# Where the queries' inverse norms are applied, and where some operands are let in, in a two-layer hybrid attention block

## The chip, the cores and the metric

The kernel runs on one core of one Trainium2 chip. The metric is device microseconds of one execution. A core has several engines that work side by side, each with its own queue of instructions: TensorE (PE in the profile; PEld is its weight loads) multiplies matrices, VectorE (DVE) and ScalarE (ACT) do elementwise work, GpSimd (POOL) does elementwise work and issues some transfers, and SyncE (SP) issues the other transfers. The engines wait for each other by semaphores. Matrix products land in PSUM banks, everything else lies in SBUF.

## The reference, cut to what matters

The input is 512 tokens of width 1024, with 16 learned meta tokens ahead of them: T = 528. Two layers run one after the other, each like this:

```python
h = rms_norm(x, norm_g)
q, k, v, gate_a, u_b, gate_b, q_idx, k_idx, w_idx, merge = split(h @ w_in)
q = rope(rms_norm(q, qn_g)); k = rope(rms_norm(k, kn_g))     # 8 heads of 64 for q, one for k and v
attn = indexer_sparse_attention(q, k, v, rope(q_idx), rope(k_idx), w_idx, k_top=128)
y_a = (attn * silu(gate_a)) @ w_a
y_b = (multiscale_pool(u_b, ...) * silu(gate_b)) @ w_b
g_a, g_b = split(sigmoid(merge))
x = x + (g_a * y_a + g_b * y_b) @ w_out
```

In `indexer_sparse_attention` eight index heads give every query a score for each key that it may see (chunks of 64 tokens, causal by chunk), the 128 keys with the largest scores are kept, and each of the eight heads does a softmax over the kept keys alone. `rms_norm(q)` divides a query of one head by its root mean square, so 1/rms is one number per token and head. Everything is float32.

## The kernel before

**Numbers.** A float32 product is made of three TensorE passes over operands split in two parts of the format float32r: high by high, low by high, high by low. So each weight and each activation appears as a high part, made by a cast on ACT (`high`, L177; `hhi`, `ahi`), and a low part, made by a subtraction of the high part on DVE (`low`; on POOL for some of `hlo`). A weight chunk is 256 columns of w_in, in two halves of 128x1024.

**Order.** TensorE and DVE execute in the order in which the program writes their instructions. ACT, POOL and SP are ordered by the framework's scheduler. The program arranges its text with four devices:

- `prep_q` is a list of steps that turn a loaded chunk into operands. `w_prep_enqueue` adds a chunk's steps; `prep_one` does the next. `group_done`, called after each group of matmuls, and `end()` in `mix_gates` take steps from it by a count. A plain chunk has three steps: `high(0)`; `low(0)` with `high(1)`; `low(1)`. Other chunks have their low parts made by an accumulating transfer of POOL (`minus`, L191 and L192, and `plus`, L196).
- `later(fn, n)` puts a step n groups of matmuls behind.
- `fill` holds generators of steps (index scores, attention) that are let in beside the dense products. They are paid by a credit which grows by a rate for each group: `R_ATT` (L30) is that rate in the attention, one number for each layer.
- `sel` holds the steps of the top-k: a maximum of eight (`dve.max`) and a replacement of these eight, 16 rounds, two query tiles interleaved. They are let in when the DVE time counted so far lies below the TensorE time counted so far. `ensure(i)`, called before the logits of query tile i, forces what is left of the top-k that this tile needs, in one burst.

**Buffers.** SBUF tiles rotate in named pools. Those that matter: "L", six buffers of 128x544 (logits `lt`, index scores `r`, split queries `qs`, pool sums `us`, the gates' weight sum, fetched sheets `hsheet`); "tt", six of 128x272 (RoPE terms `t1`, `t2`, squares `sq`, `th`, `c`, `p1`); "B", eight (split queries of the index `qi`, attention queries `qq`, `pw`, and from the fifth gate group on the gates `ta`). A tile waits until the readers of the tile that had its buffer are done.

**Stages of a layer.** Norm; key, value and index key with the first index queries; the other index queries; gate_b and pool branch; `queries(0)`, gate_a, `queries(1)`; the pool branch's output `zb` (`dense`, copied by ACT at L1148); the merge gates (`mix_gates`); the attention branch's output (`ahi`, `alo` times w_a); w_out. The index scores, the top-k and the attention are let in from the queries' stage to the end of the merge gates.

**The queries.** `q_post(t, ps, normed, dst)` (L555 on) takes one token tile's four heads from PSUM: two DVE products for RoPE; with `normed`, ACT's square (L567), a DVE sum, a DVE addition and POOL's power −1/2 (`rq`, L433) give 1/rms; POOL adds the two products (L572); one group later DVE multiplies by `rq` and ACT casts the high part (`qs`, L581), then DVE makes the low part, TensorE transposes and ACT copies to `qq` (L590).

**A unit of attention** is one tile of 128 queries and two heads; there are 16 units in a layer. `logits` does the matmuls; `soft` adds the mask and takes the minimum in one DVE instruction for each head (`lt`, `mn`; the logits come with their sign turned, so the minimum is the largest), then ACT's exponential with scale −1 and the minimum as bias (L680), summing to `sm`; `scale` takes the reciprocal `rs` on DVE, multiplies on ACT (`lt`, L691) and puts the 16 meta columns, multiplied on DVE, into `pm`; `turn` transposes on TensorE and ACT copies to `pt` (L707); `values` multiplies by v. Meta columns of all heads are multiplied in one go after a tile's fourth unit (`meta_turn`). In layer 0 the meta tokens' own attention (`meta_attn`) follows at the end.

**Merge gates.** Eight groups q = 0 to 7 of seven products each (a Strassen-like scheme over two halves of the tokens and of the width), in the order a11, a12, s2, s1, s3, s4, a22; a product is 12 matmuls. Some operands are sums of activations; two of the four sheets go to memory early and are fetched late: `fetch(w, g)` (L826, a transfer on SP), `high` (L832, ACT) and `low` (DVE), in the order fetch(1,0), fetch(1,1), high and low of both, fetch(0,0), fetch(0,1), each after a group of the `zb` stage, then `last_sum` with the high and low parts of the (0,·) pair.

**w_a.** When a query tile's attention is done, `splits` makes its `ahi` on ACT (L1161) and puts it in `alo_q`; `alos` makes all that is there on DVE. It is called in the last gate group between the product s4 and its `end()`, and after the gates. w_a's matmuls use high by high first, `alo` last.

Of the kernel before, what the change touches and what calls it, by code (L numbers as in the profile page):

```python
# [8 lines left out]
F32 = mybir.dt.float32  # L9
# [8 lines left out]
T = 528  # L18
# [8 lines left out]
HB = 272  # L27
NCOL = 968
LB = 6
R_ATT = (1.8, 1.7)  # L30
FULL = 1.0
CAP = 1.5
W0 = 3
# [54 lines left out]
def tile_block(ctx: ExitStack, tc: tile.TileContext, x, meta, w_in, pool_w, w_a, w_b, w_out, rows, hgain, c_tab, out):  # L88
# [63 lines left out]
    def w_tile():  # L152
        return wpool.tile([128, 1024], F32R, tag="w", name="w", bufs=8)

    def w_prep_enqueue(eng=dve):
        c = W["prep"]
        if c >= len(chunks):
            return
        W["prep"] += 1
        kt = chunks[c][0][0].shape[1]  # L160
        cols = 2048 // kt
        ready[c] = {}
        if c in mixed:
            prep_q.extend(mixed_prep(c))
            return
        parts = ready[c] = ([], [])

        def split(which):
            t = w_tile().rearrange("p (k e) -> p k e", e=cols)
            parts[which].extend(t[:, k] for k in range(kt // 2))  # L170
            return t

        his = {}

        def high(s):
            his[s] = split(0)
            act.copy(his[s], raws[c][s])  # L177

        def low(s):
            eng.tensor_sub(split(1), raws[c][s], f(his[s]))  # L180
            if s == 1:
                del raws[c]
                w_load()

        def second():
            low(0)
            high(1)

        def minus(s):
            t = split(1)  # L190
            act.activation(t, raws[c][s], AF.Copy, scale=-1.0)  # L191
            gp.dma_start(t, raws[c][s], accum_op=OP.add)  # L192

        def plus(s):
            t = split(0)
            act.copy(t, raws[c][s])  # L196
            if s == 1:
                del raws[c]
                w_load()

        if c in by_dma:
# [199 lines left out]
    Ck = one.tile([128, 5, 64], F32, name="Ck")  # L401
    Sk = one.tile([128, 5, 64], F32, name="Sk")
    BV = one.tile([128, 4, 2, 64], F32, name="BV")

    def small(n, name):
        return tmp.tile([128, n], F32, tag=f"sm{n}", name=name, bufs=6)
# [145 lines left out]
        later(third, 2)  # L552
        later(trans, 3)

    def q_post(t, ps, normed, dst):  # L555
        s, m = TOK[t]
        p3 = ps[:m, :256].rearrange("p (h d) -> p h d", h=4)
        t1 = tmp.tile([128, HB], F32, tag="tt", name="t1", bufs=6)
# [6 lines left out]
        if normed:  # L565
            sq = tmp.tile([128, HB], F32, tag="tt", name="sq", bufs=6)
            act.activation(sq[:m, :256], ps[:m, :256], AF.Square, scale=HD ** -0.5)  # L567
            ss = small(4, "ss4")
            dve.tensor_reduce(ss[:m], sq[:m, :256].rearrange("p (h d) -> p h d", h=4), axis=AX.X, op=OP.add)
            rq = small(4, "rq")  # L570
            inv_rms(rq[:m], ss[:m], dve)
        gp.tensor_tensor(t1[:m, :256], t1[:m, :256], t2[:m, :256], op=OP.add)  # L572
        if normed:
            qs = tmp.tile([128, 544], F32R, tag="L", name="qs", bufs=LB)[:, :512].rearrange("p (h c) -> p h c", h=4)
# [1 line left out]
            qs = tmp.tile([128, 4, 128], F32R, tag="P", name="qs", bufs=3)  # L576

        def second():
            if normed:
                dve.tensor_tensor(v1, v1, rq[:m, :, None].to_broadcast([m, 4, 64]), op=OP.mult)  # L580
            act.copy(qs[:m, :, 0:64], v1)  # L581

# [66 lines left out]
    def attention(ensure):  # L649
        st, pvs, pms = {}, {}, {}  # L650

        def logits(u):
            i, j = divmod(u, 4)
            if j == 0:
                ensure(i)
                pms[i] = tmp.tile([128, NH, 16], F32, tag="pm", name="pm")
            st[u] = []
            for hh in range(2):
                h = 2 * j + hh
                qS = QS[i, h // 4][:, h % 4, :]  # L660
                for pi, (o, w) in enumerate(KPARTS[i]):
                    ps = bank("a")
                    pe.matmul(ps[:, :w], qS, KK[:, 0, o:o + w], start=True, stop=False)
                    pe.matmul(ps[:, :w], qS, KK[:, 1, o:o + w], start=False, stop=True)
                    st[u].append((hh, pi, o, w, ps))

        def soft(u):
            i, j = divmod(u, 4)
            n = NK[i]
            mn, sm = small(2, "mn"), small(2, "sm")  # L670
            L = {}
            for hh, pi, o, w, ps in st[u]:
                if pi == 0:
                    L[hh] = tmp.tile([128, 544], F32, tag="L", name="lt", bufs=LB)
                e = min(w, n - o)
                dve.tensor_tensor_reduce(L[hh][:, o:o + e], ps[:, :e], SC[i][:, n - 1::-1] if i == 0 else SC[i][:, o:o + e], 1.0,
                                         3e38 if pi == 0 else mn[:, hh:hh + 1], op0=OP.add, op1=OP.min,
                                         accum_out=mn[:, hh:hh + 1])
            for hh in range(2):
                act.activation(L[hh][:, :n], L[hh][:, :n], AF.Exp, scale=-1.0, bias=mn[:, hh:hh + 1],  # L680
                               accum_out=sm[:, hh:hh + 1])
            st[u] = L, sm

        def scale(u):
            i, j = divmod(u, 4)
            n = NK[i]
            L, sm = st[u]
            rs = small(2, "rs")
            dve.reciprocal(rs, sm)
            for hh in range(2):  # L690
                act.activation(L[hh][:, 16:n], L[hh][:, 16:n], AF.Copy, scale=rs[:, hh:hh + 1])  # L691
                dve.tensor_scalar(pms[i][:, 2 * j + hh, :], L[hh][:, 0:16], rs[:, hh:hh + 1], None, op0=OP.mult)
            st[u] = L

        def turn(u):
# [99 lines left out]
    def sums_of_h(l, s0, n2):  # L795
# [25 lines left out]
        back = {}  # L821

        def fetch(w, g):
            t = back[w, g] = tmp.tile([128, 544], F32, tag="L", name="hsheet", bufs=LB)[:, :2 * n2].rearrange(
                "p (k c) -> p k c", k=2)
            dma(t, far[:, w, g])  # L826

        def high(w, g):
            if w == 0 and not t1_:
                t1_.append(one.tile([128, 2, 4, T // 2], F32R, tag="Alo", name="hsum1"))  # L830
            k = slice(2 * g, 2 * g + 2)
            act.copy(H[0][:, k, c1] if w else t1_[0][:, 0, k, :n2], back[w, g])  # L832

        def low(w, g):
            k = slice(2 * g, 2 * g + 2)
            hi, lo = [H[s][:, k, c1] if w else t1_[0][:, s, k, :n2] for s in range(2)]
            dve.tensor_sub(lo, back.pop((w, g)), f(hi))
# [25 lines left out]
    def mix_gates(zb, ta, s0, n2, operands, splits, alos):  # L863
        base = popped[0] - progress[W["use"]]
        end_ = [None]
        for q in range(8):
# [17 lines left out]
            def end():  # L884
                done[0] += 1
                group_done()
                while prep_q and popped[0] < base + 9 * q + LEAD + done[0] * 9 // 7:
                    prep_one()

            def gate(eh, t, src, in_sheet):  # L890
# [36 lines left out]
            total(1, 1, U, p5)  # L927
            end()
            product(S, "s4", False)
            if q == 7:  # L930
                alos()
            end()
            product(U, "a22", False)
            total(0, 1, S, u)
            gate(1, 0, U[:, :n2], False)
# [47 lines left out]
    for l in range(2):  # L983
# [20 lines left out]
        for what, t in (("q", 1), ("q", 2), ("k", 3), ("k", 4), ("q", 3), ("q", 4)):  # L1004
# [21 lines left out]
        def queries(g):  # L1026
            w = chunk()
            for t in range(0 if l == 0 else 1, 5):
# [5 lines left out]
                later(lambda t=t, ps=ps, dst=dst: q_post(t, ps, True, dst), 1)  # L1034
                group_done()


# [282 lines left out]
```

## Time and profile before

| | |
|---|---|
| median of three executions | 783.36 us (783.23 to 786.67) |
| the profiled execution | 784.69 us |
| its span | 782.9 us |
| mean granted TensorE clock | 0.997 |
| busy: TensorE, DVE, ACT, POOL | 755.2, 569.2, 468.2, 194.6 us |
| TensorE idle in the span | 27.7 us |

Times in the profile are microseconds from the start of the span, of one execution. A row of a group gives line, engine, operation, the tiles written and read by name, the shape, the count, then total busy time and mean nanoseconds of one, then the idle time of the engine just before and what ended it. Many instructions go through one recording helper and have its line, L60; they are told apart by tile. A row of the waits names the engine that waits and the work that ended the wait.

### The profile page before, as it was taken

The numbers are of one execution on the slowest core, as the hardware profiler recorded it, in microseconds if no ns is written. First come the engines' busy times: TensorE is split into PE (matmuls) and PEld (weight loads), VectorE is DVE, ScalarE is ACT, GpSimd is POOL, SyncE is SP. The second block draws the span as 40 slices with busy tenths as digits, with TensorE's granted clock in tenths as the row PEclk, the third lists the DMA queues.
The fourth block names the chain that finished last, engine by engine and source line by source line (L and its number), as shares of the span: only waits on it lengthen the run. The fifth ranks groups of instructions, "written<-read, shape, count | busy, mean of one in ns | idle before, by whom it ended". The sixth has DMA issues, their size and how long they took to land.

```text
span 782.9 us, 15738 instructions
## 1 busy us (share of the span) xinstructions
PE 755.2 (96%) x5989; PEld 717.9 (92%) x5989; DVE 569.2 (73%) x1434; ACT 468.2 (60%) x1044; POOL 194.6 (25%) x240
## 2 busy tenths in 40 slices
PE   7999999999999999899999999999999899999998
PEld 5999999999889999899999989988868899999998
DVE  6866787788897876784367568868788878858531
ACT  5677844737677787543245796555577687863420
POOL 6551164324000000053345411751400000004300
PEclk9999999999999999999999999999999999999999
DMA  9547585675022112544431678668711222127311
GB/s 297 174 103 194 141 197 136 142 196 123 28 81 83 54 56 82 158 141 136 136 109 57 161 163 206 144 148 206 175 50 55 63 85 70 56 92 234 121 57 41
DMA packets 73260, 96.95 MB, mean 124 GB/s; under 512 B 3632, under 2 KB 58192, under 8 KB 73184
## 3 DMA queue, kind: packets, MB, share of 16 engines
q1 hardware_dynamic: 67424, 74.97, 30.2%
q0 software_dynamic: 5760, 20.97, 14.7%
q8 instruction: 47, 0.77, 0.4%
q14 instruction: 29, 0.24, 0.1%
HBM read 66.41 MB, written 8.55 MB: 96 GB/s over the span
## 4 chain that ended last, share of the span: by engine, by line
PE 80%; DVE 11%; ACT 3%; POOL 2%; DMA 2%; issue 1%; SPq 0%; POOLq 0%; DVEq 0%; ACTq 0%
PE d L60 65%; PE a L60 11%; PE v L60 4%; DVE w L60 1%; DVE sc L60 1%; DVE t L60 1%; DMA hsheet<-far 1%; DVE nf L60 1%; DVE m L60 1%; POOL rq L433 1%; DVE hlo L60 1%; DVE alo L60 1%; ACT sq L567 1%; DVE ta L60 1%; DVE ss L60 0%
## 5 line engine op out<-in xcount | busy, mean ns | idle before, releaser
L60 PE MATMUL d<-hhi,w 128*128 128x256 f32 (+3 forms) x1408 | 291.4, 297 | 0.0
L60 PEld LDWEIGHTS d<-hhi,w 128*128 128x128 f32 x1408 | 227.0, 189 | 7.7 <-issue 2.3
L60 PE MATMUL d<-hlo,w 128*128 128x256 f32 (+3 forms) x704 | 193.8, 294 | 0.6 <-POOL hlo L1187 0.6
L60 PE MATMUL d<-w,hhi 128*128 128x256 f32 (+2 forms) x928 | 145.7, 286 | 3.8 <-ACT w L177 2.7
L60 PEld LDWEIGHTS d<-hlo,w 128*128 128x128 f32 x704 | 132.8, 189 | 3.2 <-POOL hlo L1187 0.8
L60 PEld LDWEIGHTS d<-w,hhi 128*128 128x128 f32 (+1 forms) x928 | 125.7, 186 | 8.0 <-ACT w L177 3.1
L60 DVE TENSOR_TENSOR w<-raw,w 128x512 fp32r<-128x512 f32 (+1 forms) x130 | 109.8, 855 | 2.7 <-ACT w L216 1.3
L1187 POOL TENSOR_TENSOR hlo<-ta,hhi 128x256 fp32r<-128x256 f32 (+1 forms) x32 | 31.3, 992 | 310.9 <-PE d L60 296.0
L60 PE MATMUL d<-w,hlo 128*128 128x256 f32 (+2 forms) x464 | 85.4, 282 | 0.0
L60 PE MATMUL d<-hsum,w 128*128 128x264 f32 (+1 forms) x576 | 78.7, 288 | 3.4 <-DVE w L60 3.4
L60 PEld LDWEIGHTS d<-hsum,w 128*128 128x128 f32 x576 | 72.9, 191 | 4.8 <-DVE w L60 3.8
L60 PEld LDWEIGHTS d<-w,hlo 128*128 128x128 f32 (+1 forms) x464 | 68.1, 187 | 0.4
L192 POOL DMA_DIRECT2D w<-raw x40 | 36.6, 934 | 101.9 <-ACT w L191 80.4
L216 ACT CAST w<-raw 128x512 fp32r<-128x512 f32 x96 | 57.0, 627 | 6.9 <-DVE raw L60 6.9
L60 DVE MATCH_REPLACE8 sc<-m,sc 128x400 f32<-128x400 f32 (+2 forms) x100 | 54.3, 549 | 0.0
L60 DVE MAX8 m<-sc 128x8 f32<-128x400 f32 (+2 forms) x100 | 52.7, 557 | 0.7
L60 PE MATMUL d<-mhi,w 128*128 128x272 f32 (+2 forms) x192 | 48.4, 330 | 0.2 <-ACT zb L1148 0.2
L191 ACT ACTIVATE w<-raw 128x1024 fp32r<-128x1024 f32 x40 | 41.4, 1059 | 8.6 <-PE d L60 8.6
L60 DVE SCALAR_TENSOR_TENSOR sc<-r,wsg,sc 128x144 f32<-128x144 f32 (+3 forms) x56 | 32.4, 582 | 16.3 <-ACT r L607 13.9
L680 ACT ACTIVATE lt<-lt,mn 128x144 f32<-128x144 f32 (+3 forms) x64 | 36.5, 574 | 10.2 <-DVE mn L60 10.2
L607 ACT ACTIVATE r<-a,wab 128x272 f32<-128x272 f32 (+2 forms) x80 | 35.8, 497 | 10.8 <-PE a L60 10.8
L196 ACT CAST w<-raw 128x1024 fp32r<-128x1024 f32 x40 | 41.5, 1054 | 0.0
(195 smaller groups left out, 1335.3 us busy)
## 6 DMA issues: line engine op xcount, KB each, us to landing
raw<-in_w_in_dram SPq DMA_DIRECT2D x72, 512.0 KB, 3.8
w<-raw POOLq DMA_DIRECT2D x40, 512.0 KB, 5.9
raw<-in_w_out_dram SPq DMA_DIRECT2D x16, 512.0 KB, 3.4
kept<-res SPq DMA_DIRECT2D x16, 264.0 KB, 2.6
res<-kept SPq DMA_DIRECT2D x16, 264.0 KB, 5.3
raw<-in_w_branch_b_dram SPq DMA_DIRECT2D x8, 512.0 KB, 4.5
raw<-in_w_branch_a_dram SPq DMA_DIRECT2D x8, 512.0 KB, 3.7
xt<-in_x_dram SPq DMA_DIRECT2D x4, 512.0 KB, 5.4
```

The lines of the kernel that those rows point to most:

```text
L60: return fn(*a, **k)
L191: act.activation(t, raws[c][s], AF.Copy, scale=-1.0)
L192: gp.dma_start(t, raws[c][s], accum_op=OP.add)
L196: act.copy(t, raws[c][s])
L216: act.copy(t[:, 0], blk[src[n]])
L433: gp.tensor_tensor(o, o, half, op=OP.pow)
L567: act.activation(sq[:m, :256], ps[:m, :256], AF.Square, scale=HD ** -0.5)
L607: act.activation(r[:, n - 1::-1] if i == 0 else r[:, o:o + e], ps[:, :e], AF.Relu, scale=wab[:, i, h:h + 1])
L680: act.activation(L[hh][:, :n], L[hh][:, :n], AF.Exp, scale=-1.0, bias=mn[:, hh:hh + 1], accum_out=sm[:, hh:hh + 1])
L1187: gp.tensor_sub(hlo[:, j, a:a + n], d, f(hhi[:, j, a:a + n]))
```

## The change

Six edits, all of them in the order or the place of work:

1. `R_ATT` of layer 0 goes from 1.8 to 1.95.
2. In one plain chunk of each layer (the one taken up after the last key tile, `("k", 4)`) both casts are one step, ahead of both low parts: `casts_first=True`.
3. For the 128-token tiles the queries are no longer multiplied by 1/rms. It is kept in `RQ` [128, 4 tiles, 8 heads], and `NR` = −`RQ` is made once for each tile. The minima are multiplied by `RQ` (one DVE instruction of 128x2 for each unit) and the exponential's scale is `NR` in place of −1. Both heads' exponentials follow that multiplication. The meta tokens' queries keep the multiplication.
4. The meta columns of `pm` are multiplied on POOL instead of DVE.
5. `fetch(0,0)` uses a buffer of "B" instead of "L"; `fetch(0,1)` two of "tt", with two transfers, two casts and two subtractions; fetch(1,·) stay in "L".
6. In the last gate group, after its fifth product, all that is left in `prep_q` is done; `alos` comes after s4's `end()` and leaves the two youngest parts for the call after the gates.

```diff
-R_ATT = (1.8, 1.7)
+R_ATT = (1.95, 1.7)
...
-    def w_prep_enqueue(eng=dve):
+    def w_prep_enqueue(eng=dve, casts_first=False):
...
+        def highs():
+            high(0)
+            high(1)
+
+        if casts_first:
+            prep_q.extend((highs, lambda: low(0), lambda: low(1)))
-        if c in by_dma:
+        elif c in by_dma:
...
+    RQ = one.tile([128, 4, NH], F32, name="RQ")
+    NR = one.tile([128, 4, NH], F32, name="NR")
...
-    def q_post(t, ps, normed, dst):
+    def q_post(t, ps, normed, dst, g=0):
...
-            inv_rms(rq[:m], ss[:m], dve)
+            inv_rms(rq[:m] if t == 0 else RQ[:, t - 1, 4 * g:4 * g + 4], ss[:m], dve)
...
-            if normed:
+            if normed and t == 0:
                 dve.tensor_tensor(v1, v1, rq[:m, :, None].to_broadcast([m, 4, 64]), op=OP.mult)
...
                 pms[i] = tmp.tile([128, NH, 16], F32, tag="pm", name="pm")
+                dve.tensor_scalar(NR[:, i], RQ[:, i], -1.0, None, op0=OP.mult)
...
+            dve.tensor_tensor(mn, mn, RQ[:, i, 2 * j:2 * j + 2], op=OP.mult)
             for hh in range(2):
-                act.activation(L[hh][:, :n], L[hh][:, :n], AF.Exp, scale=-1.0, bias=mn[:, hh:hh + 1],
+                h = 2 * j + hh
+                act.activation(L[hh][:, :n], L[hh][:, :n], AF.Exp, scale=NR[:, i, h:h + 1], bias=mn[:, hh:hh + 1],
                                accum_out=sm[:, hh:hh + 1])
...
-                dve.tensor_scalar(pms[i][:, 2 * j + hh, :], L[hh][:, 0:16], rs[:, hh:hh + 1], None, op0=OP.mult)
+                gp.tensor_scalar(pms[i][:, 2 * j + hh, :], L[hh][:, 0:16], rs[:, hh:hh + 1], None, op0=OP.mult)
...
         def fetch(w, g):
-            t = back[w, g] = tmp.tile([128, 544], F32, tag="L", name="hsheet", bufs=LB)[:, :2 * n2].rearrange(
-                "p (k c) -> p k c", k=2)
-            dma(t, far[:, w, g])
+            if (w, g) == (0, 1):
+                back[w, g] = [(slice(k, k + 1), sheet(n2, "hsheet")[:, None, :n2]) for k in (2, 3)]
+            else:
+                t = tmp.tile([128, T], F32, tag="B", name="hsheet", bufs=8) if w == 0 else sheet(T, "hsheet")
+                back[w, g] = [(slice(2 * g, 2 * g + 2), t[:, :2 * n2].rearrange("p (k c) -> p k c", k=2))]
+            for k, t in back[w, g]:
+                dma(t, far[:, w, g, k.start - 2 * g:k.stop - 2 * g])
...
-                while prep_q and popped[0] < base + 9 * q + LEAD + done[0] * 9 // 7:
+                while prep_q and (popped[0] < base + 9 * q + LEAD + done[0] * 9 // 7 or (q == 7 and done[0] > 4)):
                     prep_one()
...
             product(S, "s4", False)
+            end()
             if q == 7:
-                alos()
-            end()
+                alos(2)
...
-                w_prep_enqueue()
+                w_prep_enqueue(casts_first=True)
...
-        def alos():
-            while alo_q:
+        def alos(keep=0):
+            while len(alo_q) > keep:
```

(`high` and `low` of the fetched sheets loop over the parts that `fetch` put into `back`; `sheet(n, name)` takes a buffer of "tt" for up to 272 columns and of "L" for more.)

More of the change, by code (lines that the diff above doesn't have):

```diff
@@ L830, in high @@
                 t1_.append(one.tile([128, 2, 4, T // 2], F32R, tag="Alo", name="hsum1"))
-            k = slice(2 * g, 2 * g + 2)
-            act.copy(H[0][:, k, c1] if w else t1_[0][:, 0, k, :n2], back[w, g])
+            for k, t in back[w, g]:
+                act.copy(H[0][:, k, c1] if w else t1_[0][:, 0, k, :n2], t)
         def low(w, g):
-            k = slice(2 * g, 2 * g + 2)
-            hi, lo = [H[s][:, k, c1] if w else t1_[0][:, s, k, :n2] for s in range(2)]
-            dve.tensor_sub(lo, back.pop((w, g)), f(hi))
+            for k, t in back.pop((w, g)):
+                hi, lo = [H[s][:, k, c1] if w else t1_[0][:, s, k, :n2] for s in range(2)]
+                dve.tensor_sub(lo, t, f(hi))
         early = deque([lambda: sums(0), lambda: lows(0), lambda: sums(1), lambda: lows(1)])
@@ L1033, in queries @@
                 ps = tok_group(t, w)
-                later(lambda t=t, ps=ps, dst=dst: q_post(t, ps, True, dst), 1)
+                later(lambda t=t, ps=ps, dst=dst: q_post(t, ps, True, dst, g), 1)
                 group_done()
```

## The prediction

> **What bounds the kernel now.** I read the page first: shares of the engines and the chain that ended last.
>
> ```profile
> span 782.9 us, 15738 instructions
> PE 755.2 (96%) x5989; PEld 717.9 (92%) x5989; DVE 569.2 (73%) x1434; ACT 468.2 (60%) x1044; POOL 194.6 (25%) x240
> PE 80%; DVE 11%; ACT 3%; POOL 2%; DMA 2%; issue 1%; SPq 0%; POOLq 0%; DVEq 0%; ACTq 0%
> ```
>
> TensorE is busy in 96% of the span and the change takes no matmul away. So a gain can only come out of TensorE's idle time, 27.7 us (782.9 − 755.2), and a loss only from new waits of TensorE. The next view is therefore the waits of TensorE, layer 0 first (40 to 390 us), then layer 1 (430 us to the end); columns: total us, times, longest.
>
> ```profile
> PE d L60 <- DVE w L60: 4.0, 2, 2.4
> PE d L60 <- ACT w L177: 1.4, 1, 1.4
> PE a L60 <- DVE lt L60: 0.9, 1, 0.9
> PE a L60 <- DVE mn L60: 0.7, 1, 0.7
> ...
> PE a L60 <- DVE qs L60: 0.4, 1, 0.4
> PE d L60 <- ACT zb L1148: 0.2, 1, 0.2
> ...
> PE d L60 <- DVE w L60: 2.8, 2, 1.7
> PE a L60 <- ACT lt L691: 2.7, 1, 2.7
> PE v L60 <- ACT pt L707: 1.7, 1, 1.7
> PE d L60 <- ACT w L177: 1.4, 1, 1.4
> PE a L60 <- DVE qs L60: 0.7, 1, 0.7
> ```
>
> These eleven rows are 7.6 us in layer 0 and 9.3 us in layer 1, and all stand where the change edits. The last view is the windows, for how loaded the others are in the attention, and for the clock.
>
> ```profile
> core 0: us, PE busy (x) PEld busy (x) DVE busy (x) ACT busy (x) POOL busy (x), PEclk, DMA share, GB/s
> 215.00:246.00 31.00, 29.54 (x246) 27.97 (x247) 27.81 (x76) 22.87 (x60) 0.00 (x0) 1.00 0.23 69
> 246.00:277.00 31.00, 31.00 (x268) 29.61 (x268) 25.72 (x70) 25.73 (x64) 0.00 (x0) 1.00 0.23 69
> ...
> 216.50:222.00 5.50, 5.50 (x46) 5.19 (x47) 5.36 (x15) 4.96 (x14) 0.00 (x0) 1.00 0.31 95
> ...
> 617.00:620.30 3.30, 0.64 (x6) 0.44 (x5) 3.26 (x13) 0.56 (x2) 0.00 (x0) 1.00 0.00 0
> 620.30:624.00 3.70, 3.63 (x21) 3.44 (x22) 3.70 (x11) 3.70 (x12) 0.00 (x0) 0.71 0.03 7
> 624.00:628.00 4.00, 4.00 (x30) 3.87 (x30) 2.83 (x9) 2.64 (x7) 0.00 (x0) 0.84 0.43 131
> ```
>
> In layer 0's attention DVE and ACT have 3 to 8 us left of 31, and POOL does nothing. After the longest stall of layer 1 the granted clock is 0.71, then 0.84.
>
> **The change part by part.**
>
> *First weight casts* (the two ACT w L177 waits, 1.4 each).
>
> ```profile
> 41.56 1.04 ACT L177 CAST w<-raw 128x1024 fp32r<-128x1024 f32 x1
> 43.73 1.13 POOL L426 TENSOR_TENSOR Ck<-consts,gk 128x320 f32<-128x320 f32 x1
> 47.98 1.22 DVE L60 TENSOR_TENSOR w<-raw,w 128x1024 fp32r<-128x1024 f32 x1
> 48.48 1.07 ACT L177 CAST w<-raw 128x1024 fp32r<-128x1024 f32 x1
> 49.58 1.29 DVE L60 TENSOR_TENSOR w<-raw,w 128x1024 fp32r<-128x1024 f32 x1 [0.38 <-ACT w L177]
> ```
>
> The second cast (48.48) goes right behind the first (ending 42.60), ahead of the key's square; its matmuls then wait for no cast. In layer 0 the square, POOL's tables (Ck) and all behind them come 1.04 later, so both lows end about 1.0 later than a DVE free of the cast would have them; that is beyond what TensorE would then want. How far is not to be read here, so I take half of the wait, 0.65 (bounds 0, the second low as late as ever, and 1.4). In layer 1 there are no tables to build, and DVE waits for TensorE there: 1.4 (bounds 0.65, if the same shift bites, and 1.4).
>
> *Queries' norms and the meta columns.* Sixteen multiplications with their waits for POOL's power leave DVE; so do 64 meta-column scalings. What comes instead, 32 multiplications of 128x2 and 8 of 128x8, has no row; the nearest is the 128x2 reciprocal.
>
> ```profile
> L60 DVE TENSOR_TENSOR t<-t,rq 128x256 f32<-128x256 f32 x16 | 6.8, 423 | 6.4 <-POOL rq L433 6.3
> L60 DVE TENSOR_SCALAR pm<-lt,rs 128x16 f32<-128x16 f32 x64 | 11.9, 232 | 1.1
> L60 DVE RECIPROCAL rs<-sm 128x2 f32<-128x2 f32 x32 | 5.1, 158 | 1.7 <-ACT lt L680 1.7
> ```
>
> DVE loses 18.7 us of rows and 6.3 of waiting. A new one I put at 0.25, between the reciprocal's 0.16 and the removed 0.42 and nearer the former, whose shape it has: 40 × 0.25 = 10, so DVE gets lighter by 8.7. None of it is on the path but the 32 small ones (below, the new wait). POOL gets 32 scalings in each layer's attention; the first to need them is the meta attention after the last unit. The nearest POOL row (Ck above, 128x320, twenty times the size) takes 1.13: 32 of those, 36 us, fit into the 62 us from 215 to 277 where POOL has 0.00. Taken at nothing; uncovered, the last one would cost the meta attention at most those 1.13.
>
> On TensorE the removed multiplication takes away DVE qs, mn and ACT zb of layer 0 (0.4 + 0.7 + 0.2). But what is late next is the fetched sum:
>
> ```profile
> 188.31 3.88 DMA hsheet<-far
> ...
> 565.45 5.45 DMA hsheet<-far
> ```
>
> These are links of the chain. In layer 0 it lands at 192.2, and ACT's cast of it (L832) stands ahead of the gate's copy that TensorE needs at 193.2. Its issue waits behind a weight load on SP's queue, not on the multiplication; I take 0.3 of 1.3 (bounds 0, 1.3).
>
> *Fetched sums.* A fetched sheet moves from the "L" buffers (six, shared with the logits lt) to a "B" buffer, another to two "tt" buffers with two transfers, two casts and two subtractions. The order on SP's queue becomes fetch(1,0), then the split pair, fetch(1,1), fetch(0,0), weight loads between. The buffers wait for readers that end earlier than the loads behind them are issued, so no load is held. Layer 1: the transfer at 565.45 had a load, another sheet and a load in front, and ACT held the copies of pt behind it; now its neighbour leaves some 10 us earlier and one transfer less is ahead, landing near 569.5, where it landed at 570.9. With qs gone too I take 2.2 of 2.4 (0.7 + 1.7; bounds 0, the sheet no earlier so that pt waits for what qs gave, and 2.4).
>
> The other effect is in the logits. Two heads' logits take two "L" buffers:
>
> ```profile
> 211.81 0.44 DVE L60 CUSTOM_DVE_ANT_0 lt<-a,sc 128x272 f32<-128x272 f32 x1 [3.06 <-ACT hsum L832]
> 215.72 0.68 DVE L60 TENSOR_TENSOR w<-s,w 128x512 fp32r<-128x512 f32 x1
> ...
> 588.64 0.44 DVE L60 CUSTOM_DVE_ANT_0 lt<-a,sc 128x272 f32<-128x272 f32 x1 [2.94 <-PE a L60]
> ```
>
> DVE stood 3.06 us for a buffer, then the top-k steps and two low sums went ahead of the weight operand that TensorE waited 2.4 us for. With two buffers more the operand is ready 3.06 earlier, beyond the 2.4: gain 2.4 (bounds 0, if another buffer is short, and 2.4). In layer 1 the same: 2.94 idle against 1.1 of wait (2.8 − 1.7): 1.1 (bounds 0 and 1.1).
>
> *Faster attention, layer 0.* R_ATT 1.95 for 1.8 lets attention in about 5 products earlier at its end, so the meta attention, whose maximum stood behind other DVE work (PE a <- DVE lt), is no longer the last: 0.9 (bounds 0 and 0.9).
>
> *Top-k burst, layer 1.*
>
> ```profile
> 615.42 1.23 DVE sc L60 x3
> 616.65 1.08 DVE m L60 x2
> ```
>
> The steps forced in a burst before the third tile's attention stand in front of the reciprocal that ACT's scaling needs. DVE is lighter, so one more round is let in before, by the order in which the instructions are issued: a replacing pair (1.23) and a maximum pair (1.08) less, of which I count 1.8, since other work moves up between. The transposes also come a product of 12 matmuls later, 1.4 (46 matmuls took 5.5 us from 216.5 to 222, 0.12 each). Gain 2.5 of 2.7 (bounds 1.8, the shortened burst alone, and 2.7). The clock: windows of 3.70 and 4.00 us at 0.71 and 0.84 lost 3.70 × 0.29 + 4.00 × 0.16 = 1.7. The 2.4 us stall at 214 left it at 1.00 (216.5 to 222), so a stall of 0.2 should; 1.7 (bounds 0 and 1.7). The Trainium skill (TensorE: Matmul & The Clock Gate, What's actually happening) puts the drop after at least one idle window of about 3.4 us; by that a stall of 2.7 is too short, the drop has another cause that stays, and the sum would come out 1.7 higher, at 773.2. In this trace the drop follows the stall directly and is nowhere else in these windows, so I go by the stall.
>
> *Last operands* (w_a's alo).
>
> ```profile
> 703.34 0.23 DVE c L60
> ...
> 703.68 1.22 DVE w L60
> 704.89 2.41 DVE alo L60 x4
> 707.30 1.15 DVE w L60
> ```
>
> Before, w's second low stood behind four alo subtractions. Now both lows go first, then alo, two of them kept for after the last gate. In layer 1 the first half needs only two alo: c 0.23 and as much again for its other half, 1.22 + 1.15 + 1.2 (two alo) = 4.0, against 3.8 of TensorE work (products s4 and a22 and eight matmuls, 32 × 0.12): the wait of 1.7 shrinks to 0.2, gain 1.5 (bounds 0.3, two alo more, and 1.7). In layer 0 the first half starts at the meta columns, whose alo is last of the kept: the work to be done before is the same, it ends at the same place, the wait changes its name: 0 of 1.6 (4.0 − 2.4; bounds 0 and 0.25).
>
> *The new wait.* Both heads' exponentials now wait for both minima and the multiplication: 0.44 (the second lt) + 0.25 = 0.69 later for each of 32 units, and the reciprocal behind them on DVE too. TensorE waits for a unit's scaling in one case of 32 today (ACT lt L691). I price four units, 4 × 0.69 = 2.8 (bounds 0 and 8 units, 5.5), as DVE has only 3.2 us free of 31 in the densest window.
>
> **The sum.** Layer 0: 0.65 + 0.3 + 2.4 + 0.9 + 0 = 4.25. Layer 1: 1.4 + 2.2 + 1.1 + 2.5 + 1.7 + 1.5 = 10.4. Together 14.65, less 2.8: −11.85 us. The profiled execution took 784.69 (its span 782.9), 1.33 above the median of 783.36. I apply the sum to the median: 771.5. The ends of the bounds add to −17.25 with no new wait, and to 5.5 − 2.75, +2.75, with the most.
>
> **The rivals.**
> *Gaps come back elsewhere.* In each stall something else is late next: a low, the sheet's landing, alo. Layer 0 shows two such (0 of 1.6; 0.3 of 1.3). If that also holds for the slots (3.5), the clock (1.7) and half the last operands (0.75), 14.65 − 5.95 − 2.8 = −5.9: 777.5. For it: a sheet took 5.45 us to land. Against: the idle of 3.06 and 2.94 has its own named cause.
> *Slower, by the softmax's chain.* Each unit costs 0.69 where its transposes come before ACT is done. The gain of 14.65 is eaten from 21 units of 32 (14.65 / 0.69), and from 27 it is slower by 3.9. All 32: 22.1 − 14.65 = +7.4, 790.8. For it: at 1.95 layer 0's attention has steps 8% closer, where DVE is at 27.81 and ACT at 25.73 of 31. Against: today 31 of 32 have slack, and DVE gets lighter by 8.7 us.
> *It doesn't do what it says.* The sheets in "tt" and "B" wait for their own readers, hold SP's queue and the loads with it, and the buffers they free are taken by s2. Gains of slots, sheets and clock go (2.4 + 2.2 + 1.1 + 1.7 = 7.4) and 2.8 of waits stay: −4.5; with loads late by as much, 4.5 us, 0: 783.4.
>
> **How the numbers follow.** My forecast 771.5 gets 0.50 (own range 767 to 775.5), gaps elsewhere 0.24 (775.5 to 779.4), no effect 0.13 (779.4 to 787.3), slower 0.13 (above). A measurement here tells 0.5%, 3.9 us, from no change. So faster 0.74, same 0.13, slower 0.13. The range 767 to 783.5 leaves 0.04 below, and above it the slower case and a little of the one without effect, 0.16.
>
> **What would show it.** No wait of TensorE for ACT w L177; no DVE idle of 3 us ahead of lt; no wait for w<-s near 214 and 591; clock 1.0 near 620; the wait of layer 0's w_a named alo, not w; POOL with 64 rows of pm. It is wrong if waits of transposes for lt L691 turn up in more than eight units, or a fetched sheet lands later than 192.2 and 570.9.

## The result, and the profile after

The changed kernel took 773.78 us (median of four, 771.71 to 774.25) against 783.83 us before (median of four, 783.23 to 786.67). The ratio is 0.986, with a 95% interval from 0.983 to 0.989. The profiled execution took 774.25 us, with a span of 772.5. The forecast was 771.5 with a range of 767 to 783.5.

From the page of the changed kernel, the same three lines:

```profile
span 772.5 us, 15843 instructions
PE 754.8 (98%) x5989; PEld 718.7 (93%) x5989; DVE 557.9 (72%) x1396; ACT 475.0 (61%) x1046; POOL 235.4 (30%) x304
PE 82%; DVE 9%; ACT 5%; POOL 1%; issue 1%; DMA 1%; SPq 0%; DVEq 0%; ACTq 0%; POOLq 0%
```

TensorE works as long as before (754.8 against 755.2) and idles 17.7 us in place of 27.7. So 10.0 of the 10.4 us of span came out of TensorE's waits, as the sum supposed. POOL is busy 40.8 us longer, ACT 6.8 longer, and DVE 11.3 shorter.

The waits of TensorE in the changed kernel, layer 0 (40 to 390 us), then layer 1 (from 430 us):

```profile
PE d L60 <- DVE alo L60: 1.8, 1, 1.8
PE d L60 <- DVE w L60: 0.9, 1, 0.9
PE a L60 <- ACT pt L718: 0.7, 2, 0.5
PE d L60 <- POOL hlo L1202: 0.6, 1, 0.6
PE d L60 <- ACT zb L1163: 0.4, 1, 0.4
PE a L60 <- DVE lt L60: 0.3, 1, 0.3
...
PE a L60 <- POOL pm L703: 1.3, 1, 1.3
PE a L60 <- ACT pt L718: 0.4, 1, 0.4
PE a L60 <- DVE qs L60: 0.4, 1, 0.4
PE d L60 <- DVE alo L60: 0.3, 1, 0.3
```

Layer 0 has 4.7 us left of 8.2 (POOL hlo counted in both), layer 1 has 2.4 of 9.3. Gone are both waits for a cast, both for w<-s, the one for the transposes' lt (2.7) and the one of layer 1's value products for pt (1.7). Three rows are new in kind: POOL pm, 1.3 us; alo, 1.8 us, in layer 0 in the place of w; and waits of the logits' matmuls for pt, 0.7 and 0.4. The 0.9 for w in layer 0 is a low part of the first weight, where the cast was waited for before.

The clock, in windows of the changed kernel (columns as in the prediction: length, TensorE, its weight loads, DVE, ACT, POOL, granted clock, DMA share, GB/s):

```profile
326.00:329.30 3.30, 1.45 (x13) 1.23 (x11) 3.23 (x7) 0.82 (x2) 0.00 (x0) 1.00 0.87 256
329.30:333.00 3.70, 3.70 (x19) 3.70 (x20) 1.11 (x3) 0.42 (x1) 0.76 (x1) 0.57 1.02 357
333.00:337.00 4.00, 4.00 (x34) 4.00 (x33) 2.51 (x7) 1.78 (x3) 1.52 (x2) 0.97 0.57 214
...
613.00:614.30 1.30, 0.05 (x2) 0.05 (x2) 1.30 (x5) 0.63 (x2) 1.20 (x2) 1.00 0.00 0
614.30:618.00 3.70, 3.70 (x29) 3.65 (x29) 2.09 (x6) 3.26 (x8) 0.00 (x0) 1.00 0.37 107
```

The half clock of layer 1 is gone. In this execution there is one in layer 0 instead, behind the 1.8 us wait for alo: 3.70 × 0.43 + 4.00 × 0.03 = 1.7 us. (What the clock did at the start of the kernel stands in the last section.)

### The profile page after: what moved, and what is told of

Read it like the earlier page. It is cut to its first block, busy times and chain, and to the rows that moved or that the text cites. A ratio compares the mean times of both kernels' runs of the same rounds, so it can differ in the third digit from the quotient of the medians.

```text
span 772.5 us, 15843 instructions
## 1 busy us (share of the span) xinstructions
PE 754.8 (98%) x5989; PEld 718.7 (93%) x5989; DVE 557.9 (72%) x1396; ACT 475.0 (61%) x1046; POOL 235.4 (30%) x304
## 4 chain that ended last, share of the span: by engine, by line
PE 82%; DVE 9%; ACT 5%; POOL 1%; issue 1%; DMA 1%; SPq 0%; DVEq 0%; ACTq 0%; POOLq 0%
PE d L60 67%; PE a L60 11%; PE v L60 4%; DVE w L60 2%; DVE nf L60 1%; ACT lt L691 1%; DVE hlo L60 1%; ACT w L222 1%; DVE t L60 1%; DVE sc L60 1%; DMA hsheet<-far 1%; DVE alo L60 0%; DMA xt<-in_x_dram 0%; DVE raw L60 0%; DVE m L60 0%
## 5 line engine op out<-in xcount | busy, mean ns | idle before, releaser
L703 POOL TENSOR_SCALAR pm<-lt,rs 128x16 f32<-128x16 f32 x64 | 40.3, 644 | 183.1 <-DVE rs L60 169.2
L691 ACT ACTIVATE lt<-lt,mn,NR 128x144 f32<-128x144 f32 (+3 forms) x64 | 42.4, 665 | 12.0 <-DVE mn L60 12.0
L191 ACT ACTIVATE w<-raw 128x1024 fp32r<-128x1024 f32 x40 | 41.3, 1057 | 11.3 <-PE d L60 11.3
L580 POOL TENSOR_TENSOR t<-t,t 128x256 f32<-128x256 f32 (+1 forms) x34 | 30.8, 907 | 39.2 <-DVE t L60 39.2
```

Of the source, the lines that this page charges most:

```text
L691: act.activation(L[hh][:, :n], L[hh][:, :n], AF.Exp, scale=NR[:, i, h:h + 1], bias=mn[:, hh:hh + 1], accum_out=sm[:, hh:hh + 1])
L703: gp.tensor_scalar(pms[i][:, 2 * j + hh, :], L[hh][:, 0:16], rs[:, hh:hh + 1], None, op0=OP.mult)
```

## Experiments

The theory: each wait has its named cause, and a part is worth what its own wait was. The first rival: the gains are coupled, so that a part alone gives nothing or does another's work. The second rival is that of the prediction on the slow side: the softmax's longer chain. All runs were timed beside the kernel before, in three groups, and ratios are to the kernel before of the same group. The four runs with one part alone form the first group (before: 785.87). The changed kernel once more, meta columns on DVE, rate 1.8 and meta first form the second (785.55), and the other four the third (784.8). Times compare closely inside a group only.

### One part alone

*Norms only*: before with `RQ`, `NR`, the 128x2 multiplication and the exponential's new scale.

```diff
-            if normed:
+            if normed and t == 0:
                 dve.tensor_tensor(v1, v1, rq[:m, :, None].to_broadcast([m, 4, 64]), op=OP.mult)
...
+            dve.tensor_tensor(mn, mn, RQ[:, i, 2 * j:2 * j + 2], op=OP.mult)
```

> The kernel before with the norms' part alone (RQ, NR, the 128x2 multiplication, the exponential's scale); meta columns stay on DVE. Theory (each wait has its own named cause): the layer 0 waits for DVE mn (0.7) and qs (0.4) go, a wait for ACT zb of 0.2 to 1.2 stays behind the fetched sheet; in layer 1 qs shrinks, pt (1.7) and both w<-s waits (2.4 and 1.1) stay because buffers and transfers are as before; 1 to 2 us faster, about 782. Rival (a lighter DVE is what closes the stalls): the w<-s waits and the wait for lt of 2.7 shrink too, 5 us faster or more. Slow rival (the softmax's chain): waits for lt or pt in several units, slower than before.

Measured: 781.37, ratio 0.9944 (0.9924 to 0.9965).

*Fetched sheets only*: before with the changed kernel's `fetch`, `high` and `low`.

```diff
-            t = back[w, g] = tmp.tile([128, 544], F32, tag="L", name="hsheet", bufs=LB)[:, :2 * n2].rearrange(
+            if (w, g) == (0, 1):
+                back[w, g] = [(slice(k, k + 1), sheet(n2, "hsheet")[:, None, :n2]) for k in (2, 3)]
```

> The kernel before with the fetched sheets' part alone (B and tt buffers, split transfer). Theory: both idle times of DVE of 3 us ahead of lt and both w<-s waits (2.4 and 1.1) go, the pt wait of layer 1 (1.7) shrinks by 1 or more; 4 to 5 us faster, about 779. Rival (the buffers freed are taken at once, or the new ones wait for their readers): the w<-s waits stay and the sheets land as late as before, within 1 us of before.

Measured: 779.15, ratio 0.9934 (0.9911 to 0.9957). DVE ahead of layer 0's w<-s, in the kernel before (between the two rows that the prediction shows), then norms only, then sheets only:

```profile
212.17 1.18 DVE L60 MAX8 m<-sc 128x8 f32<-128x400 f32 x2
...
214.49 1.31 DVE L60 TENSOR_TENSOR hsum<-hsheet,hsum 128x528 fp32r<-128x528 f32 x2
```

```profile
211.04 0.44 DVE L60 CUSTOM_DVE_ANT_0 lt<-a,sc 128x272 f32<-128x272 f32 x1 [3.67 <-issue]
...
211.60 1.33 DVE L60 TENSOR_TENSOR hsum<-hsheet,hsum 128x528 fp32r<-128x528 f32 x2
212.85 0.68 DVE L60 TENSOR_TENSOR w<-s,w 128x512 fp32r<-128x512 f32 x1
```

```profile
208.25 0.44 DVE L60 CUSTOM_DVE_ANT_0 lt<-a,sc 128x272 f32<-128x272 f32 x1
...
210.31 0.69 DVE L60 MATCH_REPLACE8 sc<-m,sc 128x528 f32<-128x528 f32 x1
210.92 1.39 DVE L60 TENSOR_TENSOR hsum<-hsheet,hsum 128x528 fp32r<-128x528 f32 x3
212.22 0.68 DVE L60 TENSOR_TENSOR w<-s,w 128x512 fp32r<-128x512 f32 x1
```

With the sheets moved, the second lt follows the first with no idle time, and both waits for w<-s are gone, as the theory had it. But the norms alone also cut layer 0's wait, from 2.4 to 0.3 us, although DVE's idle time ahead of the second lt stays (3.67 us; this trace names no releaser for it). What is missing with the norms only is the top-k steps that stood between lt and the low sums: the whole top-k of these tiles had been let in by then. So the stall was made of two things in a row, the buffer (3.06) and the top-k steps behind it (2.3: from 212.17, the maximum, to 214.49, the low sums, in the kernel before), and taking either away was enough. In layer 1 the norms alone did not help this wait (1.5 in place of 1.1).

The wait for pt in layer 1 went against both expectations. It did not shrink with the sheets alone but halved with the norms alone (1.7 before); sheets only, then norms only:

```profile
PE v L60 <- ACT pt L707: 1.6, 1, 1.6
```

```profile
PE v L60 <- ACT pt L712: 0.8, 1, 0.8
```

Issue of the first sheet of layer 1, in the kernel before, with norms only and with sheets only:

```profile
562.27 1.28 SPq L826 DMA_DIRECT2D hsheet<-far  x1
```

```profile
548.97 0.45 SPq L831 DMA_DIRECT2D hsheet<-far  x1
```

```profile
559.12 1.26 SPq L830 DMA_DIRECT2D hsheet<-far  x1
```

The prediction gave the 10 us to the sheets' buffers. It is the norms that send the sheet out early. Both together take the wait to 0.9, and only the whole change removes it.

*Norms and sheets together*: the two edits above in one kernel.

> The kernel before with the norms' and the fetched sheets' parts together. Alone each removed most of layer 0's wait of 2.4 for w<-s (norms left 0.3, fetch nothing) and norms halved the pt wait of layer 1, fetch did not. Theory (that stall was made of the buffer and of top-k steps behind it, and either cure is enough): it is counted once, so together about 2 us less than the two gains added; the pt wait and both w<-s waits gone; 777 to 778. Rival (the parts add): 774 to 775.

Measured: 780.61, ratio 0.9949 (0.9932 to 0.9966); the intervals of the two parts alone and of both overlap, so both together are not told from either. The rival that parts add (774 to 775) is refuted, and the theory's 777 to 778 was 3 us too low as well. Where they don't add is seen when the start of the nth matmul is compared between traces, for each n. From 43 us to the end of layer 0 the norms gain 2.4 us, the sheets 2.7, and both together only 1.5. In layer 1, the half clock left out (1.7, which the sheets' execution happened not to have), they gain 1.4 and 1.0, and both together 2.3: there the parts add. Most of the overlap of 3.6 us in layer 0 has a name: the stall of 2.4, of which either cures 2.1 or more, and a new wait of 1.1 for the gate's copy behind the sheet's landing, in place of 0.2:

```profile
PE d L60 <- ACT zb L1157: 1.1, 1, 1.1
```

The other 0.6 us or so is in no wait of this view; it stays open.

*Casts only.*

```diff
+        if casts_first:
+            prep_q.extend((highs, lambda: low(0), lambda: low(1)))
+        elif c in by_dma:
```

> The kernel before with the casts' part alone. Theory: the layer 1 wait for the cast (1.4) goes whole; in layer 0 about 1.0 of 1.4 comes back as a wait for the low parts, since POOL's tables and what follows them move back; 1.5 to 2 us faster, about 782. Rival (both waits go whole, the later square is covered): 2.7 faster, about 781, and no wait for w lows near 50 us.

Measured: 783.91, ratio 0.9965 (0.9945 to 0.9984). No wait for a cast is left. In layer 0 a wait of 0.92 for the low part begins at 49.9 us, so the wait shrank by 0.4; the hundred matmuls around it took 12.92 us in place of 12.99, so little of that was gained. Layer 1's wait of 1.4 went whole. The waits went as the theory had it.

*Last operands only*: the flush of `prep_q` and `alos(2)` behind s4's `end()`.

```diff
             product(S, "s4", False)
+            end()
             if q == 7:
-                alos()
-            end()
+                alos(2)
```

> The kernel before with the last operands' part alone. Theory: layer 1's wait of 1.7 becomes one of 0.2 to 0.4 for alo; layer 0's wait of 1.6 stays at 1.6 to 1.9 and is for alo in place of w; 1.4 us faster, about 782.4. Rival (the flushed low parts delay the gates' own sums): new waits ahead of the gate products, no gain.

Measured: 782.94, ratio 0.9972 (0.9955 to 0.9988). Layer 1's wait is 0.27 in place of 1.70, layer 0's 1.85 in place of 1.63, and it is for alo in place of w, as the theory had it.

### The changed kernel with one part undone

The yardstick first, the changed kernel once more:

> The changed kernel once more, as the yardstick of the three beside it: 773 to 774, waits as in its first profile; the half clock near 330 (behind the wait of 1.8 for alo) may be there or not.

Measured: 773.63, ratio 0.9843 (0.9817 to 0.9870). The waits are the same, but for the gate's copy in layer 0 (0.7 in place of 0.4), and no half clock follows the wait for alo.

*Meta columns back on DVE.*

```diff
-                gp.tensor_scalar(pms[i][:, 2 * j + hh, :], L[hh][:, 0:16], rs[:, hh:hh + 1], None, op0=OP.mult)
+                dve.tensor_scalar(pms[i][:, 2 * j + hh, :], L[hh][:, 0:16], rs[:, hh:hh + 1], None, op0=OP.mult)
```

> The changed kernel with the meta columns' scaling back on DVE. Theory: the wait of 1.3 for POOL pm in layer 1 goes, nothing comes in its place since DVE has the room: about 1 us faster than the changed kernel, 772.5. Rival (the 64 scalings off DVE are part of the gain): the burst ahead of the third tile grows again, a wait for lt of 1 us or more comes back, and the time is that of the changed kernel or 1 to 2 us more.

Measured: 773.97, ratio 0.9846 (0.9819 to 0.9872), the changed kernel's. The wait for pm is gone, and one for ACT's scaling stands in its place:

```profile
PE a L60 <- ACT lt L702: 1.3, 1, 1.3
```

The rival was right, and the theory, which had 772.5, was not: moving this work to POOL buys nothing, since it takes as much as it gives.

*Layer 0's rate back at 1.8.*

```diff
-R_ATT = (1.95, 1.7)
+R_ATT = (1.8, 1.7)
```

> The changed kernel with layer 0's rate at 1.8 again. Theory: the waits for pt in layer 0 (0.5 and two of 0.15) go, the meta attention's wait for lt grows from 0.3 to 0.9; within 0.5 us of the changed kernel. Rival (the higher rate carries a part of the gain): 2 us slower than the changed kernel. Slow rival (the denser attention is the cost of the softmax's chain): 1 us faster or more.

Measured: 773.55, ratio 0.9844 (0.9822 to 0.9866). The meta attention's wait is 0.9 again and the pt waits of layer 0 are gone, as expected. The rate is worth nothing measurable. It moves layer 1 too: the wait for pm is absent there, and one of 0.6 for pt appears.

*The meta columns' last operands first*, which is a new version rather than an undoing.

```diff
         def alos(keep=0):
+            alo_q.sort()
             while len(alo_q) > keep:
```

> The changed kernel with w_a's last operands made in order of tokens, so that the 16 meta columns, which layer 0's first half needs, are no longer among the two kept. Theory: layer 0's wait of 1.8 for alo goes to 0.1 or less and with it the half clock behind it: 1.8 to 3.4 us faster than the changed kernel, about 771.5. Rival (the wait is for the weight's second low part, or the meta columns are not there in time): the wait stays above 1 us and the time with it.

The place it aims at, in the chain of the changed kernel:

```profile
324.00 2.35 DVE w L60 x2
326.35 1.80 DVE alo L60 x3
328.15 0.34 DVE c L60
328.50 0.74 DVE alo L60 x2
329.24 0.04 issue
329.29 1.74 PE d L60 x8
```

TensorE starts at 329.29 with the last two alo, of which the second is the meta columns. Measured: 771.25, ratio 0.9816 (0.9795 to 0.9837); its four times (770.87 to 771.93) lie below all four of the changed kernel beside it (772.4 to 774.33). The waits for alo of both layers together:

```profile
PE d L60 <- DVE alo L60: 0.6, 2, 0.3
```

So layer 0's 1.85 became 0.30. In its group this version beats the changed kernel by 2.4 us in the median. The 1.55 us of wait is shown; the rest may be half clocks, which come by chance, and isn't. The intervals of the two ratios overlap, and the changed kernel's fastest execution of the first result (771.71) is as fast.

### Sizes

*Meta first, and rate 1.8.*

```diff
-R_ATT = (1.95, 1.7)
+R_ATT = (1.8, 1.7)
...
         def alos(keep=0):
+            alo_q.sort()
```

> The kernel with the meta columns' last operands first, and layer 0's rate back at 1.8. With the changed kernel's other edits the rate 1.8 had no wait for POOL pm in layer 1, but one for pt of 0.6 and a longer one for the meta attention. Theory (the rate is worth nothing by itself, and its 1.95 sets the phase of layer 1): the same as meta_first within 0.8 us, 770.5 to 772. Rival: the meta attention ends too late for its columns to be taken first, and the wait of 1.8 for alo is back.

Measured: 772.22, ratio 0.984 (0.9820 to 0.9861): 0.2 above the theory's range, and no better than meta first at 1.95. By its ratio it is no better than the changed kernel either (0.9843), so the gain of meta first is not seen a second time here. The wait for alo is 0.64, and the gate's copy waits 1.1.

*Meta first, and the fourth unit's meta columns on DVE.*

```diff
-                gp.tensor_scalar(pms[i][:, 2 * j + hh, :], L[hh][:, 0:16], rs[:, hh:hh + 1], None, op0=OP.mult)
+                (dve if j == 3 else gp).tensor_scalar(pms[i][:, 2 * j + hh, :], L[hh][:, 0:16], rs[:, hh:hh + 1], None, op0=OP.mult)
```

> The kernel with the meta columns' last operands first, and the meta columns of each tile's fourth unit, which the transposes wait for, scaled on DVE, the others on POOL. Theory (POOL's scaling is held while DVE works on two operands from SBUF, and only the last one is on the path): the wait of 1.3 for POOL pm goes and leaves 0 to 0.4: 1 us faster than meta_first, 770.2. Rival (the burst ahead of it is late by as much): a wait for lt of about 1.3 in its place, as with all of them on DVE, and the same time.

Measured: 771.14, ratio 0.9826 (0.9804 to 0.9848). The wait for pm is gone from the trace and no wait for lt came, but in this execution the gate's copy of layer 0 waited 0.7 us for the sheet and pt 0.4 more; the time is not told from meta first, and the theory's 770.2 was not reached. The wait's removal is shown, its worth is not.

*A longer chain.*

```diff
             dve.tensor_tensor(mn, mn, RQ[:, i, 2 * j:2 * j + 2], op=OP.mult)
+            for _ in range(4):
+                dve.tensor_scalar(mn, mn, 1.0, None, op0=OP.mult)
```

> The changed kernel with four more dependent DVE instructions of 128x2 (a multiplication by one) between the minimum and the exponential, in each of the 32 units: 4 x 0.16 = 0.65 us longer in the softmax's chain, as much again as the change itself put there. Theory (one unit in eight is waited for): 0.65 x 4 = 2.6 us slower than the changed kernel, at most 4. Slow rival of the prediction (every unit's transposes wait for its softmax): 0.65 x 32 = 21 us slower. If the chain has slack everywhere: no change.

Measured: 779.96, ratio 0.9937 (0.9919 to 0.9955), so 6.3 us above the changed kernel's 773.6 of the second group (7.4 by the two ratios), between the two forecasts and beyond the theory's 4. The four instructions take 0.169 each, 0.68 together. Its waits:

```profile
PE a L60 <- ACT lt L704: 4.3, 2, 2.8
...
PE a L60 <- POOL pm L705: 1.4, 1, 1.4
```

It is not a cost for every unit. In layer 0, at the higher rate, no wait of note came of it (the largest is 0.4), and at the start of w_out it is no later than the changed kernel. In layer 1 two transposes wait, 1.5 us at 564 (the first unit) and 2.8 us at 613 (the burst before the third tile), and a half clock of 1.7 us follows the second. 1.5 + 2.8 + 1.7 = 6.0 of the 6.3 to 7.4. The slow mechanism exists, then, but in two places, where the top-k or the first unit leaves no slack, and 0.68 us more was enough to reach them.

## Why the prediction came out as it did

The direction and its cause were right: no matmul changed, and the waits named were the ones that went. The median lies 2.3 us above the forecast. By steps:

- *First weight casts*: forecast 0.65 and 1.4. Alone, the waits shrank by 0.4 and 1.4. Layer 1 was right; in layer 0 the matmuls came only 0.07 us sooner, near the lower bound of 0.
- *Queries' norms*: forecast 0.3 of 1.3 in layer 0, because the sheet's landing is late next. The wait left there is 0.4 in one execution of the changed kernel and 0.7 in the other, so 0.5 to 0.9 came back. The mechanism was right, the size a little low. What was missed is that the norms let the top-k in earlier, and so cure layer 0's stall as well as the buffers do.
- *Fetched sums*: 2.4 and 1.1 for the buffers were right in size; 2.2 for layer 1's sheet was right in size (2.4 down to 0.4), and wrong in cause: "its neighbour leaves some 10 us earlier" is the norms' doing.
- *Faster attention*: 0.9 forecast, 0.6 measured in the waits, and given back in waits for pt (0.7), which at 1.8 are absent: nothing in sum, as the run at 1.8 shows.
- *Top-k burst*: this step failed. Of 2.5 only 1.4 came back. The wait for lt went, and POOL pm stood in its place with 1.3. The faulty sentence is that the first to need the meta columns "is the meta attention after the last unit", with the price "at nothing". The transposes of `meta_turn` need them after every fourth unit, so the scaling has a due time in each tile, and POOL missed it once: the four transposes of lt were done at 613.0, and the second of POOL's pair ended at 614.2. At rate 1.8 the units fall otherwise and this wait is absent.
- *The clock*: 1.7 for layer 1 came, and one of 1.7 appeared in layer 0 of the same execution. The forecast took a drop as a fixed consequence of one stall. The runs show the same stall with and without it: the 1.85 us for alo was followed by a half clock in one execution of the changed kernel and not in the other; the 2.66 us stall of layer 1 was followed by one before, and by none with the sheets alone. It should have been priced at a chance. The prediction's other reading, that a stall of 2.7 us is too short for a drop, is not borne out: the drop went with the stall, and seven such drops came with stalls of 1.85 to 2.8 us (last section).
- *Last operands*: 0 and 1.5 forecast; alone −0.2 and 1.4. Right. What it read as "the same work" could be reordered, which took 1.55 us off the wait, as meta first shows.
- *The new wait*: 2.8 forecast as four units' transposes. None waits for lt in the changed kernel; four waits for pt, 0.53 + 0.15 + 0.15 + 0.43 = 1.26 (from the trace's gaps), stand in their place. What causes these stays open: norms only has one of 0.5 in layer 0 that the kernel before has not, but the long chain, longer still, has none there. The delay of 0.69 was right by luck: the multiplication took 0.16 in place of 0.25, and the exponential 0.09 more than before, which the prediction did not count (last section). The long-chain run shows that the margin left was smaller than 0.68 us in two places.

So 4.25 for layer 0 was 4.0 in waits less 1.7 of clock, and 10.4 for layer 1 was 9.0. Less 1.3 for pt, that makes 10.0 of the 10.4 us by which the span shrank. The agreement is closer than the account deserves. By the starts of the nth matmuls, the profiled execution lost 0.35 us in the first 43 us, gained 2.3 in layer 0, where the waits and the clock give 1.5, and 8.4 in layer 1, where they give 8.5; so 0.8 us of layer 0 has no name here. The rival in which gaps come back elsewhere was partly true (pm 1.3, pt 1.3, a clock drop elsewhere of 1.7), for 4.2 us in place of its 6.

## What to carry to other kernels

A stall that ends on one instruction can be two delays in a row on the engine that makes it; either cure removes it, and the two gains don't add. Work that is moved to an idle engine needs its own reader looked up: not the last one, but the first. When a wait merely changes its name after a reordering, look at which piece the waiting engine needs first, and make that one first: one `sort` took 1.55 us off a wait here.

## What the runs showed of the hardware

**POOL is held while DVE reads two operands from SBUF.** The scaling of 16 columns takes 0.63 us for a pair on POOL alone, and up to 2.8 when DVE runs instructions with two operands in SBUF beside it. POOL of the changed kernel, and then DVE at the second place:

```profile
588.87 0.63 POOL L703 TENSOR_SCALAR pm<-lt,rs 128x16 f32<-128x16 f32 x2 [8.09 <-DVE rs L60]
...
611.41 2.79 POOL L703 TENSOR_SCALAR pm<-lt,rs 128x16 f32<-128x16 f32 x2 [8.68 <-DVE rs L60]
```

```profile
611.16 0.67 DVE L60 TENSOR_TENSOR w<-s,w 128x512 fp32r<-128x512 f32 x1
611.75 0.68 DVE L60 TENSOR_TENSOR raw<-raw,s 128x512 f32<-128x512 f32 x1
612.36 0.41 DVE L60 SCALAR_TENSOR_TENSOR zb<-c,zb 128x256 f32<-128x256 f32 x1
612.69 0.42 DVE L60 SCALAR_TENSOR_TENSOR zb<-th,zb 128x256 f32<-128x256 f32 x1
613.03 0.68 DVE L60 TENSOR_TENSOR w<-raw,w 128x512 fp32r<-128x512 f32 x1
613.63 0.57 DVE L60 CUSTOM_DVE_ANT_0 lt<-a,sc 128x400 f32<-128x400 f32 x1
```

The first of the pair ends at 613.9, just after the last of five DVE instructions with two operands in SBUF (613.71); the second takes 0.3 us beside lt, one of whose operands is in PSUM. Over all 64 the mean is 644 ns, against some 330 alone. Five of the 64 took 2.5 us, each beside the same five DVE instructions, and each ended 0.2 us after the fifth. Beside shorter or looser runs POOL got through sooner, at times before the run had ended (1.25 us at 290.6). The Trainium skill (GPSIMD Engine Reference, Specifications) names this sharing with VectorE for instructions with two SBUF inputs; the trace agrees, and adds that a dense run of such instructions can hold POOL for its whole length.

**An exponential whose scale is read from a tile takes 0.09 us more than one with a constant scale.** From the profile of the kernel before and of the changed kernel:

```profile
L680 ACT ACTIVATE lt<-lt,mn 128x144 f32<-128x144 f32 (+3 forms) x64 | 36.5, 574 | 10.2 <-DVE mn L60 10.2
```

```profile
L691 ACT ACTIVATE lt<-lt,mn,NR 128x144 f32<-128x144 f32 (+3 forms) x64 | 42.4, 665 | 12.0 <-DVE mn L60 12.0
```

By width (144, 272, 400 and 528 columns) the means go from 411, 520, 630 and 736 ns to 506, 610, 716 and 826: 86 to 95 ns at each. Norms only has the same (505 to 829), so it comes with that part. This is 5.9 of the 6.8 us that ACT is busy longer.

**The half clock is a matter of phase.** It lasts some 3.4 us each time behind a stall, or longer in the first 24 us of the kernel, where it is there in some executions and not in others, on the same instructions. Windows from 12 to 24 us, before and then norms only:

```profile
12.00:24.00 12.00, 10.51 (x63) 9.25 (x62) 12.00 (x18) 7.30 (x13) 8.87 (x10) 1.00 0.76 257
```

```profile
12.00:24.00 12.00, 9.69 (x49) 8.44 (x48) 12.00 (x18) 7.05 (x13) 9.12 (x10) 0.57 0.77 261
```

By 73 us the second is 1.1 us behind, before any instruction that it changed. From 40 us on, the clock records of the traces show what the chance hangs on. Each trace's half clocks begin and end on a grid of 3.41 us whose position differs from execution to execution. What counted was how long TensorE idled inside one step of that grid:

| stall | its length | most idle time in one grid step | the next step |
|---|---|---|---|
| alos only, w<-s in layer 0 | 2.38 | 2.37 | half clock |
| before, lt in layer 1 | 2.66 | 1.93 | half clock |
| alos only, lt in layer 1 | 2.66 | 1.86 | half clock |
| changed kernel, alo in layer 0 | 1.85 | 1.85 | half clock |
| sheets only, lt in layer 1 | 2.66 | 1.88 | full clock |
| casts only, lt in layer 1 | 2.66 | 1.83 | full clock |
| before, w<-s in layer 0 | 2.37 | 1.58 | full clock |
| changed kernel once more, alo | 1.85 | 1.55 | full clock |

All seven half clocks of the fourteen traces between 40 us and the last 10 us follow a step with 1.85 us or more, and no step with less was followed by one; the 1.88 shows that the border is not sharper than that. In the first 24 us steps with 1.4 and 1.65 us were followed by a half clock too, so there the border is another. An estimate from these numbers: a stall of 2.66 us that falls anywhere on the grid has 1.85 us in one step in 0.7 of the cases (2.37 / 3.41). It was followed by a half clock in two of four. So such a stall costs its length and, by chance, 1.7 us more.
